# Splitting part of the middle stage's weights during the first feed-forward, and an output projection in two passes

## The chip, the core and the metric

The kernel runs on one core of a Trainium2 chip. The metric is the device time of one execution in microseconds. Engines: TensorE (PE, matmuls, results in PSUM), VectorE (DVE), ScalarE (ACT), GpSimd (POOL) and SyncE (SP, which here only issues DMAs). ACT issues DMAs too. Each engine works through its own queue in order, and the engines meet through semaphores.

## The reference, cut to what matters

One layer of a hybrid decoder on 264 tokens: 256 of a prompt and 8 decode tokens. All weights are float32.

```python
x = x + 0.5 * swiglu(rmsnorm(x, n1), f1g, f1u, f1d)      # first feed-forward, 2048 -> 5504 -> 2048
h = rmsnorm(x, nm)
proj = h @ w_in                                          # input projection, 2048 -> 4864
o_att, k_buf, v_buf = attend(q, k, v, sinks)             # window attention, 16 heads
o_rwkv, shift, S = rwkv_time_mix(proj[..., ATT_COLS:], ...)   # RWKV-7, 16 heads
mixed = jnp.concatenate([o_att, o_rwkv], axis=-1)
x = x + mixed @ w_out                                    # output projection, 2048 -> 2048
x = x + 0.5 * swiglu(rmsnorm(x, n2), f2g, f2u, f2d)      # second feed-forward
y = rmsnorm(x, final_norm)
```

## The kernel before, in words

**Numbers.** A float32 weight is taken apart into two parts that PE reads in its fast format (float32r): hi is the rounded weight, lo what is left. The activations are split in the same way, and each 128 x 128 weight tile meets the 264 tokens in three matmuls, hi with hi, hi with lo and lo with hi, all into one PSUM bank. `mm` (L73) issues them.

**A chunk.** Weights come in chunks of up to four tiles (`CH = 4`, 128 x 512, 256 KB). `chunk` (L115 to L124) loads a chunk with an SP DMA into `raw` (six buffers), casts it on ACT into `hi` (L122, four buffers) and subtracts on DVE into `lo` (L57 through `tt`, four buffers). `gemm` asks for the chunks of one output tile one after another and issues 12 matmuls for each. In the input projection the third chunk of each output tile (`LOP`, k = 8) has its subtraction on POOL. `chunk` runs with high priority in the planner that orders each engine's queue, so loads and splits stand as early as buffers allow. The planner works on the whole program: what stands where in a queue follows from its own estimate of time, not from the order of the Python text.

**First feed-forward** (`ffn`): 43 tiles of the hidden width in six parts; for each part the gate and up products (two times 16 k tiles, 8 chunks for each hidden tile), then the down product for 16 output tiles in two chunks each. That makes 43 x 8 + 16 x 12 = 536 chunks. `early` issues two cache copies of 1016 KB, DRAM to DRAM, on ACT's queue in the third and fourth part. At the end the residual `x` is stored to DRAM (`xsp`) and comes back before the output projection.

**Middle stage** (`mixing_body`): 38 output tiles of the input projection (`win`), four chunks each. Tiles 0 and 1 are the low-rank columns, tiles 2 to 25 the r, k and v columns of eight head pairs, tiles 26 to 37 the attention's k, v and q. After each chunk `tick` moves a list of generators on by one step: `prep` for each head pair, `chain` for each of four batches of two pairs (a triangular solve on DVE in 30 steps of two operations, with tiles going through DRAM scratch: `gm` to `sa`, `sa` to `X` and `Xt`, `Xt` to `sb`, `sb` to `TT`, all on SP's queue), `dec_rwkv` for the decode tokens, `attend` for eight head groups, and `dec_attend`.

**Output projection.** `PASS` lists which of the 16 k tiles each pass takes: six RWKV pairs, then eight attention tiles, then the last two RWKV pairs. Before each pass `drain(need(ks))` runs the generators that make its tiles; a pass with RWKV pairs also needs the decode part. In each pass every one of the 16 output tiles is a gemm over the pass's k tiles, and DVE adds its result to the residual; in the last pass each residual tile is also split and squared for the next norm. Six k tiles make chunks of four and two, two make one chunk of two: 80 chunks in all. The rows of `w_out` are laid out on the host in the order of `PASS`.

Of the kernel before, what the change touches and what calls it, by code (L numbers as in the profile page):

```python
# [7 lines left out]
F32 = mybir.dt.float32  # L8
F32R = mybir.dt.float32r
AF = mybir.ActivationFunctionType  # L10
ALU = mybir.AluOpType
AX = mybir.AxisListType

P = 128
# [4 lines left out]
KD = 16  # L19
# [8 lines left out]
CH, NRAW, NHL = 4, 6, 4  # L28
# [5 lines left out]
LOP = (8,)  # L34
PW = (2, 1, 3, 2, 2)
ALPHA = math.exp(-0.5)
LKV = 26
SEQ = [("b", i) for i in range(4)] + [("kv", i) for i in range(4)] + [("q", i) for i in range(8)]
PASS = [[0, 1, 2, 3, 4, 5], [8, 9, 10, 11, 12, 13, 14, 15], [6, 7]]

VG1, VGM, VG2, VGF = 0, 16, 32, 48
VMU, VKK, VKA, VA0, VRK, VLW, VLB, VSK, VSD = 64, 90, 98, 106, 114, 122, 130, 138, 154
# [4 lines left out]
def body(tc, I, O):  # L47
    nc = tc.nc
    V, A, G, TE, SP = nc.vector, nc.scalar, nc.gpsimd, nc.tensor, nc.sync
    cnt = [0]  # L50

    def uid(s):
        cnt[0] += 1
        return f"{s}{cnt[0]}"

    def tt(e, out, a, b, op):
        return e.tensor_tensor(out=out, in0=a, in1=b, op=op)  # L57
# [32 lines left out]
    def pause(n):  # L90
        for _ in range(n):
            yield

    with ExitStack() as ctx:
        cp = ctx.enter_context(tc.tile_pool(name="cp", bufs=1))
        sp = ctx.enter_context(tc.tile_pool(name="sp", bufs=1))
        wp = ctx.enter_context(tc.tile_pool(name="wp", bufs=1))
        pp = ctx.enter_context(tc.tile_pool(name="pp", bufs=1, space=bass.MemoryType.PSUM))
        dp = ctx.enter_context(tc.tile_pool(name="dp", bufs=1, space=bass.MemoryType.DRAM))
# [12 lines left out]
        def mp():  # L112
            return pp.tile([P, 512], F32, tag="m", bufs=NM, name=uid("m"))

        def chunk(src, n, e, ahead=True):  # L115
            w = n * P
            with tc.high_priority() if ahead else nullcontext():
                raw = wp.tile([P, CH * P], F32, tag="raw", bufs=NRAW, name=uid("raw"))
                hi = wp.tile([P, CH * P], F32R, tag="hi", bufs=NHL, name=uid("hi"))
                lo = wp.tile([P, CH * P], F32R, tag="lo", bufs=NHL, name=uid("lo"))  # L120
                SP.dma_start(raw[:, :w], src)
                A.copy(hi[:, :w], raw[:, :w])  # L122
                tt(e, lo[:, :w], raw[:, :w], hi[:, :w].bitcast(F32), ALU.subtract)
            return hi, lo  # L124

        def gemm(ps, src, xs, step=None, rng=None, pool=False, ahead=True):
            n = len(xs)
            for k0 in range(0, n, CH):
                k1 = min(n, k0 + CH)
                if rng and k0 not in rng:  # L130
                    continue
                hi, lo = chunk(src[:, k0 * P:k1 * P], k1 - k0, G if pool and k0 in LOP else V, ahead)
                for k in range(k0, k1):
                    xh, xl = xs[k]
                    c = slice((k - k0) * P, (k - k0 + 1) * P)
                    mm(ps[:, :T], hi[:, c], xh, k == 0, False)
                    mm(ps[:, :T], hi[:, c], xl, False, False)
                    mm(ps[:, :T], lo[:, c], xh, False, k == n - 1)
                if step:
                    step()  # L140

        vec = cp.tile([P, NVEC], F32, name="vec")
        C = cp.tile([P, 640], F32, name="C")
# [54 lines left out]
        def ffn(nrm, xr, gu, dn, nxt, load=None):  # L198
            rstd = None
            f0 = 0  # L200
            for pi, nf in enumerate(PARTS):
                hs = [None] * nf
                late = []
                if load:
                    early(pi)
                first = load and pi == 0
                if first:
                    banks = [acc() for _ in range(NACC)] + [mp() for _ in range(NM)]
                    n0 = len(banks) // 2
                    for k in range(CH):  # L210
                        load(k)
                    for k0 in range(0, KD, CH):
                        xs = nrm.xs + [None] * (KD - len(nrm.xs))
                        for i, ps in enumerate(banks):
                            gemm(ps, gu[i // 2, i % 2], xs, rng=(k0,), ahead=False)
                            if i >= len(banks) - CH and k0 + CH < KD:
                                load(k0 + CH + i - len(banks) + CH)
                    for f in range(n0):
                        raw = [tmp(), tmp()]
                        V.tensor_copy(raw[0], banks[2 * f][:, :T])  # L220
                        A.copy(raw[1], banks[2 * f + 1][:, :T])
                        late.append((f, *raw))
                for f in range(f0 + n0 if first else f0, f0 + nf):
                    pgu = [acc(), acc()]
                    if first and f == n0:
                        sq = iter(range(KD))

                        def step():
                            for k in [x for _, x in zip(range(2), sq)]:
                                nrm.square(xr[k], k % 2, True)  # L230
                    else:
                        step = None
                    for ps, w in zip(pgu, (gu[f, 0], gu[f, 1])):
                        gemm(ps, w, nrm.xs, step)
                    last = f == f0 + nf - 1
                    if rstd is None:
                        rstd = nrm.rstd(tmp())
                    late.append((f, *(x[:, :T] for x in pgu)))
                    now = [late.pop()] + late[:(len(late) if last else 1)]
                    late = [] if last else late[1:]  # L240
                    for j, pg, pu in now:
                        E = V if last else G
                        g = tmp()
                        tt(V, g, pg, rstd, ALU.mult)
                        s = tmp()
                        act(s, g, AF.Silu)
                        u = tmp()
                        tt(V, u, pu, rstd, ALU.mult)
                        tt(E, u, u, s, ALU.mult)
                        hi, lo = tmp(dt=F32R), tmp(dt=F32R)  # L250
                        A.copy(hi, u)  # L251
                        tt(E, lo, u, hi.bitcast(F32), ALU.subtract)
                        hs[j - f0] = (hi, lo)
                if pi == len(PARTS) - 1:
                    nrm.xs = None
                for o in range(KD):
                    ps = acc()
                    gemm(ps, dn[o, :, f0 * P:(f0 + nf) * P], hs)
                    stt(xr[o], ps[:, :T], 0.5, xr[o], ALU.mult, ALU.add)
                    if pi == len(PARTS) - 1:  # L260
                        nxt(o)
                f0 += nf

        def first_ffn(n2):
            n1 = Norm(VG1)
            xr = []
            A.dma_start(vec, I["vec"])
            def load(k0):
                n1.split(xr[k0], k0 >= CH)

            def nxt(o):
                n2.split(xr[o])
                n2.square(xr[o])
                A.dma_start(xsp[o], xr[o])

            with tc.tile_pool(name="f1", bufs=1) as fp:
                cur[0] = (fp, NH)
                for q in range(4):
                    xg = fp.tile([P, 4, T], F32, tag="x", bufs=4, name=uid("x"))
                    for j in ((0, 2), (2, 4)) if q == 0 else ((0, 4),):  # L280
                        A.dma_start(xg[:, j[0]:j[1]], I["xT"][:, q * 4 + j[0]:q * 4 + j[1], :])
                    xr += [xg[:, j] for j in range(4)]
                ffn(n1, xr, I["gu1"], I["dn1"], nxt, load)

        def mixing(n2, n3):
            with tc.tile_pool(name="mx", bufs=1) as mx:
# [3 lines left out]
        def mixing_body(mx, n2, n3):  # L290
# [29 lines left out]
            mixed = [None] * 16  # L320
            have = [False]

            def win(t):
                ps = acc()
                gemm(ps, I["win"][t], n2.xs, tick, pool=True)
                if not have[0]:
                    n2.rstd(rs)
                    have[0] = True
                return ps
# [486 lines left out]
            for kind, i in SEQ:  # L816
# [10 lines left out]
                elif kind == "kv":  # L827
                    w, p = i // 2, i % 2
                    ps = win(LKV + i)
# [34 lines left out]
            k0 = 0  # L864
            for pi, ks in enumerate(PASS):
                drain(need(ks))
                for k in ks:
                    split(k)
                for o in range(KD):
                    ps = acc()  # L870
                    gemm(ps, I["wout"][o, :, k0 * P:(k0 + len(ks)) * P], [mixed[k] for k in ks], tick)
                    with tc.high_priority():
                        tt(V, xr[o], ps[:, :T], xr[o], ALU.add)
                    if pi == len(PASS) - 1:
                        n3.split(xr[o])
                        n3.square(xr[o])
                for k in ks:
                    mixed[k] = None
                k0 += len(ks)
# [132 lines left out]
```

## Time and profile before

| what | value |
|---|---|
| three runs, median (lowest to highest) | 2129.2 us (2127.75 to 2129.91) |
| the profiled execution | 2127.34 us, of which the span from first to last instruction is 2125.2 |
| granted PE clock, mean over the span | 0.970 |
| busy share of the span | PE 96%, DVE 63%, ACT 49%, POOL 20% |
| data moved | 356.27 MB, 168 GB/s on average |

The stages by their own times: the first loads of the input projection are issued at 757.7 us, its last at 1124.1, and the second feed-forward begins at about 1366.

```profile
0.00:757.00 757.00, 747.09 (x6114) 745.82 (x6115) 453.00 (x768) 373.28 (x672) 91.99 (x94) 1.00 0.59 188
757.00:1140.00 383.00, 354.57 (x3182) 332.25 (x3180) 297.16 (x657) 205.44 (x425) 190.84 (x326) 0.96 0.47 136
...
1250.00:1366.00 116.00, 112.51 (x947) 108.54 (x947) 81.14 (x164) 62.09 (x134) 17.99 (x27) 0.99 0.54 171
1366.00:2125.00 759.00, 745.63 (x6125) 744.80 (x6123) 435.87 (x736) 365.96 (x651) 94.09 (x91) 0.99 0.55 178
```

Each line is a stretch of time (from, to, length in us), the busy us of PE, of PE's weight loads, DVE, ACT and POOL with their instructions, the share of the PE clock that was granted, the mean busy share of the 16 DMA engines and the GB/s that they moved. A group line, as the prediction shows them, gives the code line, engine, operation, the tile written and the tiles read, the count, and then the busy us, the mean ns of one, the idle time of the engine just before them and what ended it. A wait line gives the engine and line that waited, for whom, the total us, how often and the longest.

### The profile page before, as it was taken

How to read it: one execution, taken by the hardware profiler on the slowest of the kernel's cores; microseconds unless marked ns; L12 is line 12 of the kernel's file. 1: busy time of each engine (PE TensorE's matmuls, PEld its weight loads, DVE VectorE, ACT ScalarE, POOL GpSimd, SP SyncE). 2: the span in 40 equal slices, each digit the busy share in tenths (PEclk: the TensorE clock that was granted, in tenths of full speed). 3: DMA queues.
4: the chain of work that ended last, by engine and by line, in shares of the span. 5: the costliest groups of instructions: out<-in, count | busy, mean ns of one | idle time of the engine just before them, and what ended most of it. 6: DMA issues, size and time to landing. Idle time of an engine off the chain costs nothing.

```text
span 2125.2 us, 45168 instructions
## 1 busy us (share of the span) xinstructions
PE 2043.9 (96%) x16870; PEld 1995.4 (94%) x16870; DVE 1334.3 (63%) x2551; ACT 1045.8 (49%) x2002; POOL 419.5 (20%) x581
## 2 busy tenths in 40 slices
PE   8999999999999999989996899999999999999997
PEld 8999999999999999888885679899999999999997
DVE  5765555556555677766888646755555565555555
ACT  5644444444444566546542344644444444444445
POOL 0301011010201146533454201220110102011012
PEclk9999999999999999989997579999999999999999
DMA  6565565656555574434343145456555565555554
GB/s 224 176 182 182 175 205 175 207 180 183 181 177 185 185 227 139 122 96 135 112 136 114 41 138 186 156 182 181 181 175 187 177 184 181 177 186 176 186 176 140
DMA packets 227532, 356.27 MB, mean 168 GB/s; under 512 B 42176, under 2 KB 83152, under 8 KB 227280
## 3 DMA queue, kind: packets, MB, share of 16 engines
q1 hardware_dynamic: 221616, 344.72, 51.8%
q10 hardware_dynamic: 5696, 8.66, 1.1%
q8 instruction: 132, 2.16, 0.4%
q14 instruction: 88, 0.72, 0.1%
HBM read 345.15 MB, written 10.21 MB: 167 GB/s over the span
## 4 chain that ended last, share of the span: by engine, by line
PE 86%; DVE 7%; DMA 2%; ACT 1%; issue 1%; POOL 1%; SPq 1%; DVEq 0%; POOLq 0%; ACTq 0%
PE acc L73 79%; PE m L73 6%; DVE lo L57 1%; DMA raw<-in_gu 1%; DVE Xt L57 1%; DVE st L57 1%; ACT L67 1%; DVE ld L57 0%; ACT t L67 0%; DMA sb<-Xt 0%; DVE s L60 0%; DVE t L57 0%; DMA TT<-sb 0%; DVE TT L57 0%; DVE t L64 0%
## 5 line engine op out<-in xcount | busy, mean ns | idle before, releaser
L73 PE MATMUL acc<-s,hi 128*128 128x264 f32 x7072 | 1317.5, 286 | 10.0 <-ACT hi L122 8.3
L57 DVE TENSOR_TENSOR lo<-raw,hi 128x512 fp32r<-128x512 f32 (+1 forms) x1266 | 861.7, 684 | 600.6 <-ACT hi L122 578.7
L122 ACT CAST hi<-raw 128x512 fp32r<-128x512 f32 (+2 forms) x1304 | 780.5, 602 | 909.5 <-PE acc L73 830.6
L73 PEld LDWEIGHTS acc<-s,hi 128*128 128x128 f32 x7072 | 1108.8, 190 | 17.8 <-ACT hi L122 8.5
L73 PE MATMUL acc<-s,lo 128*128 128x264 f32 x3536 | 1016.1, 288 | 12.7 <-DVE lo L57 10.5
L73 PEld LDWEIGHTS acc<-s,lo 128*128 128x128 f32 x3536 | 669.9, 189 | 18.5 <-DVE lo L57 14.1
L73 PE MATMUL acc<-t,hi 128*128 128x264 f32 x2752 | 502.7, 284 | 1.6 <-ACT t L251 1.6
L73 PEld LDWEIGHTS acc<-t,hi 128*128 128x128 f32 x2752 | 426.0, 188 | 1.9 <-ACT t L251 1.8
L57 POOL TENSOR_TENSOR t<-t,t 128x264 f32<-128x264 f32 (+1 forms) x162 | 173.0, 1068 | 1209.6 <-ACT hi L122 897.6
L73 PE MATMUL acc<-t,lo 128*128 128x264 f32 x1376 | 388.2, 284 | 0.0
L73 PEld LDWEIGHTS acc<-t,lo 128*128 128x128 f32 x1376 | 258.2, 188 | 0.0
L57 DVE TENSOR_TENSOR t<-acc,t 128x264 f32<-128x264 f32 x164 | 70.9, 433 | 36.7 <-PE acc L73 36.5
L57 POOL TENSOR_TENSOR s<-s,s 128x264 f32<-128x264 f32 (+1 forms) x56 | 49.5, 886 | 195.8 <-ACT s L67 179.1
L57 POOL TENSOR_TENSOR lo<-raw,hi 128x512 fp32r<-128x512 f32 x38 | 49.7, 1308 | 57.4 <-ACT hi L122 57.2
L67 ACT ACT_TABLE_LOAD x42 | 53.9, 1283 | 1.9 <-PEq L1004 1.2
L60 DVE SCALAR_TENSOR_TENSOR s<-acc,s 128x264 f32<-128x264 f32 x96 | 40.7, 428 | 16.8 <-PE acc L73 16.3
L60 DVE SCALAR_TENSOR_TENSOR x<-acc,x 128x264 f32<-128x264 f32 x96 | 40.6, 427 | 10.9 <-PE acc L73 10.4
L57 DVE TENSOR_TENSOR st<-X,Xt 128x60 f32<-128x60 f32 (+10 forms) x120 | 36.1, 300 | 10.1 <-DMA Xt<-sa 7.4
L67 ACT ACTIVATE t<-t 128x264 f32<-128x264 f32 x94 | 40.0, 425 | 3.3 <-DVE t L57 1.8
L57 DVE TENSOR_TENSOR Xt<-Xt,st 128x60 f32<-128x60 f32 (+10 forms) x120 | 36.7, 305 | 1.7
L251 ACT CAST t<-t 128x264 fp32r<-128x264 f32 x86 | 35.5, 413 | 3.6 <-POOL t L57 2.1
L73 PE MATMUL m<-s,hi 128*128 128x264 f32 x160 | 30.1, 287 | 0.4 <-ACT hi L122 0.4
(209 smaller groups left out, 1116.5 us busy)
## 6 DMA issues: line engine op xcount, KB each, us to landing
raw<-in_gu SPq DMA_DIRECT2D x688, 256.0 KB, 3.2
raw<-in_dn SPq DMA_DIRECT2D x224, 256.0 KB, 2.7
raw<-in_win SPq DMA_DIRECT2D x152, 256.0 KB, 3.2
raw<-in_dn SPq DMA_DIRECT2D x160, 192.0 KB, 2.7
raw<-in_wout SPq DMA_DIRECT2D x48, 256.0 KB, 3.0
raw<-in_wout SPq DMA_DIRECT2D x32, 128.0 KB, 2.4
xsp<-x ACTq DMA_DIRECT2D x16, 132.0 KB, 3.5
s<-xsp SPq DMA_DIRECT2D x16, 132.0 KB, 3.0
```

What stands on the lines that cost most here:

```text
L57: return e.tensor_tensor(out=out, in0=a, in1=b, op=op)
L60: return V.scalar_tensor_tensor(out=out, in0=a, scalar=s, in1=b, op0=op0, op1=op1)
L67: return A.activation(out=out, in_=in_, func=f, **k)
L73: TE.matmul(out, lhsT, rhs, start=start, stop=stop, **k)
L122: A.copy(hi[:, :w], raw[:, :w])
L251: A.copy(hi, u)
```

## The change

Of the middle stage's weight chunks 104 are split during the first feed-forward, written to DRAM as hi and lo side by side, and read back as such where they are needed.

- `hi` and `lo` of a chunk become one tile `hl` (four buffers as before).
- `presplit` is a generator over 72 chunks of the input projection (tiles 2 to 25, k = 0, 4 and 12; not k = 8, whose subtraction is on POOL) and the second chunk of each output tile in both output passes (2 x 16). For each it loads 256 KB into `praw` (three buffers) on SP, casts on ACT and subtracts on DVE into `phl` (three buffers), and stores 512 KB from ACT's queue into a DRAM tile of its own. `gemm` moves it on by one step for each chunk of the first feed-forward, and an item takes four steps (`PSTEP`).
- `chunk` with `done` given loads the 512 KB straight into `hl` on SP's queue: no `raw`, no cast, no subtraction.
- `PASS` has two passes of eight k tiles in place of three: all RWKV pairs, then attention. That makes 64 chunks, all of four tiles.

```diff
+PRE, PREK = range(2, 26), (0, 4, 12)
+PSTEP = 4
-PASS = [[0, 1, 2, 3, 4, 5], [8, 9, 10, 11, 12, 13, 14, 15], [6, 7]]
+PASS = [[0, 1, 2, 3, 4, 5, 6, 7], [8, 9, 10, 11, 12, 13, 14, 15]]
...
-        def chunk(src, n, e, ahead=True):
+        def chunk(src, n, e, ahead=True, done=None):
             w = n * P
             with tc.high_priority() if ahead else nullcontext():
-                raw = wp.tile([P, CH * P], F32, tag="raw", bufs=NRAW, name=uid("raw"))
-                hi = wp.tile([P, CH * P], F32R, tag="hi", bufs=NHL, name=uid("hi"))
-                lo = wp.tile([P, CH * P], F32R, tag="lo", bufs=NHL, name=uid("lo"))
-                SP.dma_start(raw[:, :w], src)
-                A.copy(hi[:, :w], raw[:, :w])
-                tt(e, lo[:, :w], raw[:, :w], hi[:, :w].bitcast(F32), ALU.subtract)
+                hl = wp.tile([P, 2, CH * P], F32R, tag="hl", bufs=NHL, name=uid("hl"))
+                hi, lo = hl[:, 0], hl[:, 1]
+                if done is not None:
+                    SP.dma_start(hl[:, :, :w].bitcast(F32), done)
+                else:
+                    raw = wp.tile([P, CH * P], F32, tag="raw", bufs=NRAW, name=uid("raw"))
+                    SP.dma_start(raw[:, :w], src)
+                    A.copy(hi[:, :w], raw[:, :w])
+                    tt(e, lo[:, :w], raw[:, :w], hi[:, :w].bitcast(F32), ALU.subtract)
             return hi, lo
...
+        def presplit(fp):
+            todo = [("win", t, k, CH) for t in PRE for k in PREK]
+            k0 = 0
+            for ks in PASS:
+                if len(ks) > CH:
+                    todo += [("wout", o, k0 + CH, len(ks) - CH) for o in range(KD)]
+                k0 += len(ks)
+            for i, (nm, t, k, n) in enumerate(todo):
+                w = n * P
+                raw = fp.tile([P, CH * P], F32, tag="praw", bufs=3, name=uid("praw"))
+                hl = fp.tile([P, 2, CH * P], F32R, tag="phl", bufs=3, name=uid("phl"))
+                tc.keep_in_program_order(SP.dma_start(raw[:, :w], I[nm][t, :, k * P:k * P + w]))
+                A.copy(hl[:, 0, :w], raw[:, :w])
+                tt(V, hl[:, 1, :w], raw[:, :w], hl[:, 0, :w].bitcast(F32), ALU.subtract)
+                d = dp.tile([P, 2, w], F32, tag=f"pre{i}", name=f"pre{i}")
+                A.dma_start(d, hl[:, :, :w].bitcast(F32))
+                ready[nm, t, k] = d
+                yield from pause(PSTEP)
...
-                hi, lo = chunk(src[:, k0 * P:k1 * P], k1 - k0, G if pool and k0 in LOP else V, ahead)
+                done = ready.get((pre[0], pre[1], pre[2] + k0)) if pre else None
+                hi, lo = chunk(src[:, k0 * P:k1 * P], k1 - k0, G if pool and k0 in LOP else V, ahead, done)
...
+                for g in side:
+                    next(g, None)
...
+                side.append(presplit(fp))
                 ffn(n1, xr, I["gu1"], I["dn1"], nxt, load)
+                for _ in side.pop():
+                    pass
...
-                gemm(ps, I["win"][t], n2.xs, tick, pool=True)
+                gemm(ps, I["win"][t], n2.xs, tick, pool=True, pre=("win", t, 0))
...
-                    gemm(ps, I["wout"][o, :, k0 * P:(k0 + len(ks)) * P], [mixed[k] for k in ks], tick)
+                    gemm(ps, I["wout"][o, :, k0 * P:(k0 + len(ks)) * P], [mixed[k] for k in ks], tick,
+                         pre=("wout", o, k0))
```

More of the change, by code (lines that the diff above doesn't have):

```diff
@@ L126, in gemm @@
-        def gemm(ps, src, xs, step=None, rng=None, pool=False, ahead=True):
+                hl = wp.tile([P, 2, CH * P], F32R, tag="hl", bufs=NHL, name=uid("hl"))
[7 more added lines that the diff above has]
+                    tt(e, lo[:, :w], raw[:, :w], hi[:, :w].bitcast(F32), ALU.subtract)
@@ new lines, in chunk @@
+            return hi, lo
+        ready = {}
+        side = []
+        def presplit(fp):
[16 more added lines that the diff above has]
+                yield from pause(PSTEP)
@@ L127, in gemm @@
+        def gemm(ps, src, xs, step=None, rng=None, pool=False, ahead=True, pre=None):
             n = len(xs)
```

## The prediction

> **What bounds the kernel now.** I read four views: busy time by stage, what TensorE (PE) waited for, the costliest groups, and the DMA rows. Columns of the stages: window, its length, then busy us (instructions) of PE, weight loads, VectorE (DVE), ScalarE (ACT), GpSimd (POOL), then the granted PE clock, the DMA engines' busy share and GB/s.
>
> ```profile
> core 0: us, PE busy (x) PEld busy (x) DVE busy (x) ACT busy (x) POOL busy (x), PEclk, DMA share, GB/s
> 100.00:600.00 500.00, 498.22 (x4094) 497.53 (x4093) 287.56 (x486) 234.51 (x413) 52.80 (x49) 1.00 0.58 185
> ...
> 760.00:1000.00 240.00, 225.31 (x1871) 212.91 (x1871) 171.93 (x344) 136.22 (x271) 122.08 (x231) 0.94 0.48 138
> 1000.00:1140.00 140.00, 126.27 (x1290) 116.35 (x1288) 122.66 (x309) 66.95 (x150) 67.81 (x94) 0.98 0.46 131
> 1140.00:1250.00 110.00, 84.06 (x510) 64.02 (x509) 67.14 (x228) 39.02 (x123) 24.64 (x43) 0.61 0.23 65
> ...
> 860.00:880.00 20.00, 15.29 (x116) 13.49 (x116) 19.64 (x47) 6.68 (x14) 14.31 (x27) 0.99 0.42 130
> ```
>
> Both feed-forwards are PE-bound at full clock: 4094 matmuls in 500 us is 0.122 us each, so a chunk of four weight tiles (12 matmuls) takes 1.465 us. The middle stage is where time can be won: from 760 to 1000 PE is idle 14.7 us and the clock of 0.94 costs another 225.3 x 0.06 = 13.5 us. Where a chain's triangular solve runs (860 to 880) DVE is full and PE starves. After 1000 come the input chunks 26 to 37, which the change does not pre-split, and from 1140 the last chain and attention, where DVE is not full and the clock is low: latency, which the change does not touch.
>
> What PE waited for between 760 and 1000 (total us, times, longest):
>
> ```profile
> PE m L73 <- DVE gm L57: 5.3, 4, 3.1
> PE acc L73 <- DVE lo L57: 4.3, 3, 3.1
> PE m L73 <- DVE Xt L57: 2.8, 1, 2.8
> PE acc L73 <- POOL lo L57: 1.9, 2, 1.5
> ```
>
> The splits are named only for 4.3 us; gm and Xt are chain steps that share DVE's queue with splits. From 740 to 1370 the split groups cost (busy us, mean ns, idle before):
>
> ```profile
> L57 DVE TENSOR_TENSOR lo<-raw,hi 128x512 fp32r<-128x512 f32 x183 | 140.0, 769 | 53.6 <-ACT hi L122 49.2 <-PE m L73 2.0
> L122 ACT CAST hi<-raw 128x512 fp32r<-128x512 f32 x221 | 135.3, 619 | 156.3 <-PE acc L73 130.9 <-DVE st L57 5.7 <-DVE t L57 5.6
> ```
>
> DMA: size and time to landing, then stretches of the first feed-forward and of the last output pass.
>
> ```profile
> raw<-in_win SPq DMA_DIRECT2D x152, 256.0 KB, 3.2
> sa<-gm SPq DMA_DIRECT2D x32, 16.0 KB, 2.1
> ...
> DMA to landing us min/median/max: 2.8/3.2/4.8
> ...
> 10.00:15.00 5.00, 4.66 (x30) 4.66 (x31) 1.90 (x4) 1.64 (x5) 0.00 (x0) 1.00 1.03 407
> 15.00:20.00 5.00, 5.00 (x43) 5.00 (x42) 4.46 (x9) 4.73 (x10) 0.00 (x0) 1.00 0.51 157
> ...
> 278.00:280.00 2.00, 2.00 (x18) 2.00 (x18) 0.15 (x1) 0.00 (x0) 0.00 (x0) 1.00 0.31 133
> ...
> 282.00:284.00 2.00, 1.78 (x13) 1.48 (x13) 1.42 (x3) 1.59 (x3) 0.00 (x0) 1.00 0.73 209
> ...
> 1350.00:1355.00 5.00, 3.85 (x25) 2.97 (x23) 5.00 (x11) 4.89 (x12) 3.07 (x4) 1.00 0.59 204
> ```
>
> The third line is for `raw<-in_win` alone. A full DMA moved 407 GB/s; PE near 283 us ran out once, behind a 1 MB cache copy issued at 271.7; the short last output pass is DVE-bound (5.00 of 5).
>
> **The first feed-forward.** 104 items are added, one per four chunks, so they end after 416 of 536 chunks, 610 us. One item: a 256 KB load on SP, an ACT cast (0.62), a DVE subtract (0.69 in this stage), a 512 KB store issued on ACT (0.33, as a load's issue). Per 5.86 us ACT goes from 47% to 63%, DVE from 58% to 69%. PE stays covered: a split starts when the chunk four earlier frees its buffer, 5.86 us ahead, and needs 0.62 + 0.69; the 4.5 us left is what an ACT wait for an item's load, or for DVE before its store, may take. Queued behind such a wait are the next casts, and behind them PE. POOL's queue gets nothing. Cost 0.
>
> DMA demand goes from 185 GB/s by (256 + 512) KB per 5.86 us = 134 to 319 GB/s. Against 407 that is 78%; by the share that bytes take in this stage (0.58 for 185) it would be 1.00. The full-load row is nearer, since queued loads run back to back there; 78%, cost 0, with rival B for the other end. The two cache copies of 1 MB fall into these 610 us; in the first one DVE and ACT had nothing to split for 4 us (278 row) and PE lost 0.2. With 78% behind it the backlog lasts longer: 1 MB at 407 GB/s is 2.6 us, the most that each can cost if nothing hides it; I take 1 each: +2 (0 to +5).
>
> Start: ACT is nearly full from 15 to 20 (4.73 of 5), and two items (2 x 0.95) come into it, with their loads (0.65 each at 407) ahead of chunks 1 and 5 in SP's queue: +1.5 (0 to +4).
>
> **The input projection, chunks of tiles 2 to 25.** 72 splits leave: 72 x 0.769 = 55 us of DVE's 172, 72 x 0.62 = 45 of ACT's 136. The 4.3 us on lo go. Of gm and Xt (8.1) I take two thirds, because DVE is full just where they occur: 5.4. That is 9.7 of 14.7 idle; the same share of the slow clock would be 9, and I take half, 4.5, since chain matmuls also run in slow spells. Together -14 (0 to -28, all idle and clock). In the built program the chains stand some four chunks earlier among the gemms than before, which agrees but proves nothing.
>
> The new wait: each of the 72 loads is 512 KB straight into one of the four matmul buffers, and SP issues it only when PE has freed that buffer. Before, six raw buffers ahead of four split ones gave ten chunks of cover; now it is four. A turn of a buffer takes 1.465 (PE) + 0.33 (issue) + landing. Landing: 3.2 for 256 KB, plus 256 KB at 407 GB/s = 0.65, so 3.9; from the minimum 3.5, from the maximum 5.5. At 3.9 a turn is 5.7, under PE's 5.86 for four chunks: no cost. The fourth chunk of each tile (POOL's) keeps its raw buffers and is loaded six tiles ahead. What is behind the wait in SP's queue matters too: the chain stores and reloads (gm to scratch, scratch to X, Xt, TT) stand between two of these loads. Such a group waits 2.1 for a landing and issues eight DMAs (2.6): 4.7 + 3.9 = 8.6 against 7.3, the five chunks that PE has left when the last buffer before the group came free: 1.3 late, five times in this range, half covered by chain matmuls: +3 (0 to +14.5 at 5.5).
>
> **Output projection.** The number of big matmuls stays (16 x 16 x 3). Both versions drain the last chain before the first pass in the built order, so merging heads 6 and 7 into pass one adds no wait. The last pass of two k tiles, 0.73 us of PE against two DVE passes and a split each, goes: PE idle from 1340 to 1365 is 3.3 us (3.85 of 5 in the row): -3.3 (-5 to 0). Half the chunks are then loaded split, on two of the four buffers; at 5.7 a turn no cost. After that the second feed-forward is untouched.
>
> **Sum.** +2 + 1.5 - 14 + 3 - 3.3 = -10.8. The profiled execution took 2127.3 (span 2125.2 and 2.1 around it): 2116.5. It lies 1.9 under the median of the runs, 2129.2, so I predict 2118.
>
> **Rivals.** A, the other side: landing under load. From 4.1 us a turn exceeds 5.86. At 4.7, halfway from median to maximum, the output passes (16 turns, no chain matmuls in between) lose 16 x 0.64 = 10 and the five SP groups 5 x 2.1 = 10.5; the input tiles, spaced 6.6 us or more by their issue times, lose nothing. In place of my +3 that is +21: 2136. At 5.5 it is 23 + 14.5 + 5.5 for eight dense tiles: 2158. The gain is eaten from about 4.4 us. For it: the maximum of 4.8, and a buffer that was ten chunks deep. Against it: the median, and a mean DMA share of 0.48 here. The Trainium skill (DMA: Bandwidth & Descriptors, section Latency and other measured facts) speaks for A: HBM access takes 0.2 us on average and 2 us at high load, so by its figures landing would grow by up to 1.8, an estimate of 5.7 us and a time beyond A's far end; the trace bears it out only in part, 2.8 to 4.8 for the same load.
>
> B: the first feed-forward becomes DMA-bound (share 1.00 by its own bytes). A shortfall of 2% over 610 us is 12, and the copies cost 2.6 each instead of 1: +15 on my sum: 2133. Against it: 407 GB/s.
>
> C: chain latency, not DVE's queue, makes gm, Xt and the slow clock; then only 4.3 of the 14 comes: 2128. For it: lo is named for little. Against it: DVE at 19.64 of 20.
>
> **How the numbers follow.** Forecast 0.50, A 0.23, C 0.17, B 0.10. About 0.2% (4.3 us) can be told from no change, so faster 0.50, same 0.17 (C), slower 0.33 (A and B). The forecast's own range is 2104 to 2125; with A up to a landing of 5.0 (15 + 12 + 1.6 in place of 3: 2144) and C and B inside, 2100 to 2146.
>
> **What would show it.** PE at 1.00 and fully busy from 100 to 740, DMA share near 0.8 there (near 1.0 with splits waiting for raw: B). Between 760 and 1000 few waits on gm, Xt and lo (C if they stay). Waits of PE on DMA hl: a few us in total, landing near 3.9 (A if tens of us, above all in the output passes). No DVE-full stretch at the end of the output projection. I am wrong if the middle is not shorter by some 12 us or the first feed-forward grows by more than 6.

## The result, and the profile after

The changed kernel takes 2200.4 us (median of four runs, 2196.04 to 2205.25), against 2128.9 for the kernel before: ratio 1.0333, 95% interval 1.0317 to 1.0349. The forecast was 2118, and the range ended at 2146. The profiled execution took 2199.5, with a span of 2197.7; 72.5 us of span came on top. By the start times of matmuls in the two traces they came like this:

| stretch | before | after | difference |
|---|---|---|---|
| first feed-forward, to its last down product | 767.4 us | 844.5 us | +77.1 |
| from there to the second feed-forward's first down product | 683.2 us | 677.0 us | -6.2 |
| from there to the last down product | 659.6 us | 661.2 us | +1.6 |

So the first feed-forward, costed at nothing but a slower start and two copies, lost twelve times what the middle gained. The stretches below are the first feed-forward, then the four of the middle that the prediction began with, each 77 us later than before, and the last output pass. Columns as before.

```profile
core 0: us, PE busy (x) PEld busy (x) DVE busy (x) ACT busy (x) POOL busy (x), PEclk, DMA share, GB/s
100.00:600.00 500.00, 465.33 (x3643) 453.43 (x3642) 304.18 (x517) 238.80 (x443) 36.59 (x40) 0.98 0.87 287
...
837.00:1077.00 240.00, 220.68 (x1875) 207.16 (x1874) 118.72 (x273) 96.59 (x204) 106.04 (x232) 0.97 0.68 211
1077.00:1217.00 140.00, 129.38 (x1281) 119.85 (x1281) 125.25 (x308) 64.65 (x145) 70.09 (x94) 0.98 0.48 140
1217.00:1327.00 110.00, 91.41 (x522) 69.06 (x520) 66.72 (x228) 37.33 (x120) 26.38 (x44) 0.60 0.26 76
1327.00:1443.00 116.00, 115.30 (x993) 112.76 (x992) 56.22 (x105) 44.55 (x94) 17.42 (x26) 1.00 0.76 244
```

From 100 to 600 PE issued 3643 matmuls where it had issued 4094: 11% of its work is missing, while DVE (61%), ACT (48%) and the DMA engines (share 0.87) all have time left. A stretch that slows with nothing full is one where something waits in turns.

In the input projection DVE fell from 172 to 119 us, as meant, and the clock rose from 0.94 to 0.97; yet the 240 us hold 1875 matmuls against 1871. What PE waited for there:

```profile
PE acc L75 <- DMA hl<-pre: 15.0, 11, 3.2
PE m L75 <- DVE st L59: 2.0, 1, 2.0
PE m L75 <- DVE gm L59: 1.5, 1, 1.5
```

The waits on lo, gm and Xt (12.4 us before) are down to 1.5, with 2.0 on `st`, another step of the chain; 15.0 us of waits for the read-backs stand in their place.

Now the first feed-forward. What ACT waited for from 20 to 680 us of the changed kernel (total us, times, longest):

```profile
ACT phl L146 <- DMA praw<-in_win: 127.4, 55, 5.3
ACT phl L146 <- DMA praw<-in_wout: 61.9, 29, 4.4
ACT hl L127 <- PE acc L75: 49.5, 76, 1.3
ACT hl L127 <- DMA raw<-in_gu: 19.7, 14, 6.6
```

Before, ACT's large wait, from 100 to 740, was for PE to free a buffer: it was ahead, and the wait was slack.

```profile
ACT hi L122 <- PE acc L73: 312.9, 411, 3.8
```

Now 189.3 us go into the cast of an item that waits for its own load. One turn of it, in ACT's queue and in SP's (start, us, instruction; in brackets the idle time before it and what ended it), and PE in the same microseconds:

```profile
537.54 1.02 ACT L127 CAST hl<-raw 128x512 fp32r<-128x512 f32 x2
542.97 0.62 ACT L146 CAST phl<-praw 128x512 fp32r<-128x512 f32 x1 [4.42 <-DMA praw<-in_wout]
543.50 0.61 ACT L127 CAST hl<-raw 128x512 fp32r<-128x512 f32 x1
```

```profile
537.24 0.79 SPq L145 DMA_DIRECT2D praw<-in_wout  x1
538.13 7.15 SPq L126 DMA_DIRECT2D raw<-in_dn  x4
545.33 0.59 SPq L145 DMA_DIRECT2D praw<-in_wout  x1
```

```profile
536.00:540.00 4.00, 4.00 (x35) 4.00 (x34) 3.03 (x6) 1.90 (x5) 0.00 (x0) 1.00 0.87 287
540.00:544.00 4.00, 2.62 (x22) 2.40 (x20) 0.38 (x1) 1.03 (x2) 0.00 (x0) 1.00 0.73 243
```

The item's load goes out at 537.2 to 538.0. ACT has two casts left ahead of that item's, and then stands still until 543. While it stands, no chunk is cast, DVE has nothing to subtract (0.38 of 4 us), so no raw buffer comes free and SP needs 7.15 us for four loads that take 0.33 each to issue. The next item's load is behind those four, at 545.3, and is late in its turn: ACT waits for it too, until 549.5. PE runs dry at 540 to 544, and the DMA engines, at 243 GB/s, have room to spare. The Trainium skill (Perfetto Trace Analysis, section Tensor Engine Instruction) says that ACT and DVE take their instructions strictly first in, first out; the trace agrees: the cast at 543.50 starts only when the late one, 0.53 us earlier, is under way.

The loss grows as long as there are items. By the issue times of the chunk loads in the two traces, the changed kernel is 25 us behind at chunk 100, 45 at 200, 58 at 300 and 76 at 400; after 420, with the last item done, it stays at 77 to 78.

The DMA rows of the changed kernel from 100 to 600 us (KB, median us to landing) show why an item's load is not there in time:

```profile
raw<-in_gu SPq DMA_DIRECT2D x187, 256.0 KB, 5.3
pre<-phl ACTq DMA_DIRECT2D x78, 512.0 KB, 4.2
...
praw<-in_win SPq DMA_DIRECT2D x57, 256.0 KB, 5.5
...
praw<-in_wout SPq DMA_DIRECT2D x22, 256.0 KB, 5.9
```

Over the whole run an item's 256 KB land in 5.6 us (median; 4.2 to 11.5). The chunks' own loads have slowed too, from 3.2 us in the same stretch of the kernel before to 5.3, but six raw buffers let SP send them far ahead of their casts. In the built order an item's cast stands 3.7 chunk casts behind its load on the mean (1 to 6; 3.8 by the order in the trace), 5.4 us at PE's 1.465 a chunk. Distance here counts the chunk casts that ACT does between the freeing of the raw buffer that the last load ahead of the item's goes into and the item's cast.

### The profile page after: what moved, and what is told of

The parts are those of the page before. It is cut to its first block, busy times and chain, and to the rows that moved or that the text cites. A ratio compares the mean times of both kernels' runs of the same rounds, so it can differ in the third digit from the quotient of the medians.

```text
span 2197.7 us, 44956 instructions
## 1 busy us (share of the span) xinstructions
PE 2078.3 (95%) x16870; PEld 2011.3 (92%) x16870; DVE 1342.5 (61%) x2519; ACT 1020.4 (46%) x1984; POOL 372.4 (17%) x581
## 4 chain that ended last, share of the span: by engine, by line
PE 65%; DMA 17%; DVE 10%; ACT 3%; issue 3%; SPq 1%; POOL 0%; ACTq 0%; DVEq 0%; POOLq 0%
PE acc L75 59%; DMA praw<-in_win 8%; PE m L75 6%; DVE hl L59 3%; DMA praw<-in_wout 3%; DMA hl<-pre 2%; DMA raw<-in_gu 2%; ACT hl L127 1%; ACT phl L146 1%; DVE st L59 1%; DVE Xt L59 1%; DVE t L59 1%; DVE x L62 0%; DMA raw<-in_win 0%; DMA Xt<-sa 0%
## 5 line engine op out<-in xcount | busy, mean ns | idle before, releaser
L75 PE MATMUL acc<-s,hl 128*128 128x264 f32 x10608 | 1359.7, 288 | 58.9 <-ACT hl L127 30.6
L75 PEld LDWEIGHTS acc<-s,hl 128*128 128x128 f32 x10608 | 1321.5, 190 | 82.4 <-ACT hl L127 34.8
L59 DVE TENSOR_TENSOR hl<-raw,hl 128x512 fp32r<-128x512 f32 x1146 | 812.0, 716 | 446.5 <-ACT hl L127 438.3
L127 ACT CAST hl<-raw 128x512 fp32r<-128x512 f32 (+1 forms) x1184 | 706.7, 605 | 712.4 <-PE acc L75 577.5
L75 PE MATMUL acc<-t,hl 128*128 128x264 f32 x4128 | 515.2, 286 | 18.1 <-ACT hl L127 11.3
L75 PEld LDWEIGHTS acc<-t,hl 128*128 128x128 f32 x4128 | 507.7, 189 | 24.5 <-ACT hl L127 13.4
L59 POOL TENSOR_TENSOR t<-t,t 128x264 f32<-128x264 f32 (+1 forms) x162 | 135.2, 834 | 1305.4 <-DVE t L59 891.4
L59 DVE TENSOR_TENSOR phl<-praw,phl 128x512 fp32r<-128x512 f32 x104 | 72.4, 696 | 173.7 <-ACT phl L146 163.8
L146 ACT CAST phl<-praw 128x512 fp32r<-128x512 f32 x104 | 64.4, 620 | 191.9 <-DMA praw<-in_win 129.7
L59 POOL TENSOR_TENSOR hl<-raw,hl 128x512 fp32r<-128x512 f32 x38 | 49.9, 1312 | 77.2 <-ACT hl L127 69.4
```

The source lines that it names most:

```text
L75: TE.matmul(out, lhsT, rhs, start=start, stop=stop, **k)
L146: A.copy(hl[:, 0, :w], raw[:, :w])
```

## The experiments

The theory, Q in the expectations: the cast of an item stands too close behind its load in ACT's queue, and SP's queue closes the loop. Its rival there, theory D: the DMA engines became the bound (the prediction's rival B).

**The passes alone.** The kernel before, with the two passes.

```diff
-PASS = [[0, 1, 2, 3, 4, 5], [8, 9, 10, 11, 12, 13, 14, 15], [6, 7]]
+PASS = [[0, 1, 2, 3, 4, 5, 6, 7], [8, 9, 10, 11, 12, 13, 14, 15]]
```

> The kernel before with the output projection in two passes, nothing split early. If the third pass of two k tiles cost what its idle PE showed, the time falls by 3.3 us (ratio 0.9985, 0.9975 to 1.000) and PE has no idle stretch at the end of the output projection. If merging the last two RWKV tiles into the first pass makes that pass wait for the last chain, it rises instead (over 1.002).

Measured: 2126.28 against 2129.51, ratio 0.9982 (0.9973 to 0.9991), by the ratio 3.8 us less. The term of -3.3 holds.

**The cast pinned.** The changed kernel; the item's cast is held at its place in the program's order, as its load is.

```diff
-                A.copy(hl[:, 0, :w], raw[:, :w])
+                tc.keep_in_program_order(A.copy(hl[:, 0, :w], raw[:, :w]))
```

> The changed kernel with one edit: the cast of an early item is kept where it stands in the program, six chunks behind the load's neighbours instead of 3.7 on average. Same bytes, same instructions. Theory Q (queue loop): ACT stands in its queue waiting for an item's load that was issued too shortly before, and while it waits the next loads are not issued; then the first feed-forward ends at 768 to 780 us instead of 844, and the time is 2125 to 2140. Theory D (DMA-bound: 319 GB/s is more than the DMA engines give beside this work): it still ends at 830 or later and the time stays above 2185.

Measured: 2128.86, ratio 0.9997 (0.9986 to 1.0007); the first feed-forward ends at 778.4. One moved instruction per item takes back 66 of the 77 us. Up to the end of the first feed-forward nearly all else stands as it did: apart from the items' own instructions SP's 544 chunk loads are in the same order in both traces, and so is POOL's queue; of ACT's 712 other instructions 34 have moved, of DVE's 783 it is 12. In the built order the cast now stands 6.0 chunk casts behind its load, 8.8 us. The same stretch, and what ACT waited for from 20 to 680, in this kernel:

```profile
100.00:600.00 500.00, 494.95 (x4046) 493.51 (x4046) 345.44 (x570) 275.74 (x498) 40.69 (x50) 1.00 0.95 321
```

```profile
ACT hl L127 <- PE acc L75: 181.1, 247, 5.4
ACT hl L127 <- DMA raw<-in_gu: 37.3, 31, 5.9
...
ACT phl L146 <- DMA praw<-in_win: 4.2, 11, 0.6
```

ACT waits for PE again, and the DMA engines move 321 GB/s, more than in the slow kernel: their limit was not reached there. The item loads landed no sooner (5.9 us median); the distance to the cast decided, not the load.

**No store.** The changed kernel without the store to DRAM; the middle stage splits all its chunks itself.

```diff
-                d = dp.tile([P, 2, w], F32, tag=f"pre{i}", name=f"pre{i}")
-                A.dma_start(d, hl[:, :, :w].bitcast(F32))
-                ready[nm, t, k] = d
```

> The changed kernel whose early items are loaded and split but not stored; the middle stage splits all its chunks itself. It leaves out the 512 KB stores and the reading back. DMA demand in the first feed-forward is 230 GB/s instead of 319. The cast of an item stands only 2.4 chunks behind its load here. Theory Q: ACT still waits for item loads, and the first feed-forward still ends late, 785 to 830 us. Theory D: it ends at 767 to 772 as before.

Measured: one time, 2257.63; the first feed-forward ends at 918.5. Two thirds of the added bytes are gone, and the loss has doubled: Q's direction, and further than either theory had it. An item's load lands sooner here (4.4 us median), but without the store the built order puts the cast only 2.4 chunk casts, 3.5 us, behind it:

```profile
100.00:600.00 500.00, 436.44 (x3202) 412.93 (x3201) 255.99 (x451) 204.94 (x395) 40.60 (x44) 0.96 0.60 182
```

```profile
ACT phl L146 <- DMA praw<-in_win: 218.8, 67, 7.2
```

At a DMA share of 0.60 the stretch loses 22% of its matmuls. So the loss here is not a bound in the DMA engines.

**The traffic alone.** The item's load and a store of the same size from a constant tile, without cast and subtraction; the middle stage splits all its chunks itself.

```diff
-                A.copy(hl[:, 0, :w], raw[:, :w])
-                tt(V, hl[:, 1, :w], raw[:, :w], hl[:, 0, :w].bitcast(F32), ALU.subtract)
...
-                A.dma_start(d, hl[:, :, :w].bitcast(F32))
-                ready[nm, t, k] = d
+                tc.keep_in_program_order(A.dma_start(d, full))
```

> The changed kernel with the DMA traffic of the early items alone: 104 loads of 256 KB and 104 stores of 512 KB of a constant tile at the same pace, no casts and no subtractions of them; the middle stage splits all its chunks itself. Theory Q: the first feed-forward ends at 768 to 778 us. Theory D: at 830 or later, as in the changed kernel.

Measured: one time, 2121.41 (below the kernel before, since the two passes and the one tile for hi and lo are in it); the first feed-forward ends at 777.3, at 319 GB/s:

```profile
100.00:600.00 500.00, 494.15 (x4029) 492.92 (x4028) 295.30 (x479) 229.12 (x406) 37.87 (x48) 0.99 0.94 319
```

The added traffic as such costs 10 us of the 77. Mean distance in chunk casts against loss of the first feed-forward is now a series: 2.4 and 151 us, 3.7 and 77, 6.0 and 11. In time the cast stands 3.5, 5.4 and 8.8 us behind a load that lands in 4.4, 5.6 and 5.9. The three kernels differ in more than this distance (the first has no store), but rival B is out as the cause of the 77.

Two more, to see what the read-backs cost in the middle.

**A ring of five.** The pinned kernel with five matmul buffers, paid for with two raw buffers, and each item's load issued an item ahead.

```diff
-CH, NRAW, NHL = 4, 6, 4
+CH, NRAW, NHL = 4, 4, 5
...
-                raw = fp.tile([P, CH * P], F32, tag="praw", bufs=3, name=uid("praw"))
+                if i + 1 < len(todo):
+                    fetch(i + 1)
+                raw = raws[i]
```

> The kernel with the pinned cast, with five matmul buffers instead of four, four raw buffers instead of six (the memory of one for the other), and an item's load issued one item ahead, so that its cast keeps its distance. Theory H (in the dense input tiles the read-back halves come just in time: a turn of four buffers is longer than PE's four chunks): PE's waits on the read-back fall from 15 us to under 7, tiles 2 to 9 take 57 to 59 us instead of 62, and the time is 3 to 8 us under the pinned cast's. Rival S (what holds the loads is SP's queue, with the chain's stores and reloads, not the number of buffers): waits and time stay within 2 us.

Measured: 2188.09, ratio 1.0277 (1.0255 to 1.03), where theory H had it 3 to 8 us under the pinned kernel. Two results in one. PE's waits on read-backs fall from 15.4 us in the pinned kernel to 4.1, and the middle (measured as in the table below) from 618.9 to 609.2. But the first feed-forward ends at 845.2: here ACT waits for the chunks' own loads.

```profile
ACT hl L127 <- DMA raw<-in_gu: 179.3, 135, 8.6
ACT hl L127 <- DMA raw<-in_dn: 83.9, 66, 3.4
```

Its item casts stand 8 chunk casts behind their loads, so this is another cause than the changed kernel's. Four raw buffers are too few under the added traffic, though the second feed-forward, with the same four and without it, loses nothing.

**From tile 10.** The pinned kernel; tiles 2 to 9, which PE runs through without chain work in between, keep their own splits (80 items).

```diff
-PRE, PREK = range(2, 26), (0, 4, 12)
+PRE, PREK = range(10, 26), (0, 4, 12)
```

> The kernel with the pinned cast, with input tiles 10 to 25 split early instead of 2 to 25: 80 items instead of 104. Theory H: tiles 2 to 9 fall back to 56 to 58 us from 62, the rest keeps its gain, and the time falls by 4 to 7 us against the pinned cast. Rival R (relief of DVE and ACT in tiles 2 to 9 is worth as much as the read-back costs): no change there, the time within 2 us.

Measured: 2120.87, ratio 0.996 (0.9945 to 0.9975). Tiles 2 to 9 go from 61.9 to 56.4 us, and the waits on read-backs from 15.4 to 9.9. The dense tiles were dearer with read-backs than with their own splits.

The first feed-forward still lost 9 to 11 us: by when each raw load was issued, in the pinned kernel some 6 by chunk 60, and the rest where the two cache copies run.

**A late start, copies at the end.** The pinned kernel; the items begin 32 chunks later, and both copies stand in the sixth part, behind the last item.

```diff
+            yield from pause(PWAIT)
...
-            elif pi in (2, 3):
-                nm, ck = (("ks", "ck"), ("vs", "cv"))[pi - 2]
+            elif pi == 5:
+                for nm, ck in (("ks", "ck"), ("vs", "cv")):
```

> The kernel with the pinned cast, with the first item 32 chunks later and both 1 MB cache copies after the last item instead of among them. Theory T (what is left of the first feed-forward's loss, 11 us, is the start and the two copies that meet the added traffic): it ends at 768 to 771 us instead of 778, the time is 7 to 11 us lower, 2118 to 2122. Rival U (the loss is spread over the whole stage, by the traffic as such): the end moves by less than 3 us.

Measured: 2126.16, ratio 0.9985 (0.9973 to 0.9997), the end at 776.2: a move of 2 us, which by the number is rival U's outcome. By the issue times it is not U's mechanism: until chunk 450 the items cost 2 to 3 us; then the two copies, back to back and with no item beside them, cost 7.

**Late start and from tile 10.** Both edits above.

> The late start and the input tiles from 10 on together. By theories H and T the gains add: 2112 to 2118 us, ratio to before 0.992 to 0.995. If U or R holds, 2122 to 2130.

Measured: 2116.76, ratio 0.9941 (0.9924 to 0.9957), as expected in the time. But the first feed-forward ends at 777.9, no sooner than the pinned kernel's (the copies, back to back, cost 8 here).

**Copies apart.** The last kernel with one copy in the fifth part and one in the sixth (`elif pi in (4, 5)`).

> Late start, input tiles from 10 on, and the two 1 MB cache copies in the fifth and sixth part of the first feed-forward, after the last item (80 items end by chunk 352, the copies are issued from about 360 and 448) and 88 chunks apart. If the 7 us that the copies cost in the late start came of their standing back to back, the first feed-forward ends at 768 to 772 us and the time is 2107 to 2113. If a copy costs its 2.6 us and more wherever it stands, it ends at 774 or later and the time stays at 2114 to 2119.

Measured: 2114.06, ratio 0.9918 (0.9899 to 0.9937); the first feed-forward ends at 771.0, 3.6 over the kernel before. The end is where it was expected, the time 1 us above its range.

**Five buffers, copies apart.** The last kernel with `NHL` of 5, and raw buffers taken from each stage's own memory: six in the feed-forwards, four in the middle.

> The same with five matmul buffers, and the raw buffers given by each stage's own memory: six in the feed-forwards, four in the middle stage. By theory H the waits on the read-back fall under 5 us from 11 and the middle stage is 2 to 6 us shorter than with four. Against it: the raw buffers of a stage can be filled only when the memory of the stage before is free, which can cost some us at each change of stage; then it is slower than the copies apart by 2 us or more.

Measured: 2117.38, ratio 0.9936 (0.9918 to 0.9955). No gain, and the expectation's caution is what happened. PE's waits on read-backs are 5.1 us against 7.9 with the copies apart, and the first feed-forward ends sooner (768.2). But the raw buffers now belong to the stage: the input projection's first loads are issued at 771.05, after that end, and PE starts on it 6.7 us after its last down product, where it was 0.1. So the input projection begins 3.8 us later in all.

**No items at all.** The changed kernel with an empty list of items: what is left of the change is the two passes, and hi and lo in one tile.

```diff
+            todo = []
```

> The changed kernel with no early item at all: two passes, and hi and lo of a chunk in one buffer. If the early split is worth what the waits on DVE showed (some 9 us net in the middle), this is at the two passes' time, 2124 to 2128. If the middle stage is set by chain latency and a favourable order, and the early split buys nothing, it is as fast as the best version with items, 2108 to 2118.

Measured: 2108.82, ratio 0.9892 (0.987 to 0.9915). By its median it is the fastest of all the kernels (its interval overlaps that of the copies apart): no version above has a gain that its side edits, the two passes and the one tile, don't give alone. What PE waited for in it from 770 to 1010:

```profile
PE acc L75 <- DVE hl L59: 5.3, 3, 2.9
PE m L75 <- DVE N L59: 2.9, 1, 2.9
PE m L75 <- DVE TN L540: 1.9, 2, 1.7
PE m L75 <- DVE gm L59: 1.6, 2, 1.1
```

The waits on lo (here `hl` from DVE) are as before, since every chunk is split on the spot. Those on gm (5.3 before) and Xt (2.8) are down to 1.6, but `N` and `TN`, later steps of the same chain, take 4.8: the chain's waits have moved more than they have gone, and this view does not show where the gain comes from.

**One tile alone.** The kernel before with hi and lo of a chunk in one tile, three passes.

```diff
-                hi = wp.tile([P, CH * P], F32R, tag="hi", bufs=NHL, name=uid("hi"))
-                lo = wp.tile([P, CH * P], F32R, tag="lo", bufs=NHL, name=uid("lo"))
+                hl = wp.tile([P, 2, CH * P], F32R, tag="hl", bufs=NHL, name=uid("hl"))
+                hi, lo = hl[:, 0], hl[:, 1]
```

> The kernel before, three passes, with hi and lo of a chunk in one buffer and nothing else. Two passes gave a ratio of 0.998 alone and 0.989 together with the one buffer. If the gain is the one buffer's (hi and lo freed together, so the planner sets another order), the ratio here is 0.989 to 0.994. If the two only work together, it is 0.996 to 1.002.

Measured: 2119.67 against 2128.92, ratio 0.9965 (0.9951 to 0.9978): within the range of "only together", at its lower end, and yet a gain clear of none.

The middle of these kernels, by matmul times of one profiled execution each (us; single executions of one kernel differ by some us, and that of the passes alone was the fastest of its runs). "To tile 2" ends with the first matmul of tile 2 and so holds PE's wait for the first read-back, 3.15 us in the changed kernel:

| stretch | before | after | passes alone | one tile alone | no items | copies apart |
|---|---|---|---|---|---|---|
| to tile 2 | 12.6 | 15.9 | 12.6 | 12.6 | 12.6 | 12.6 |
| tiles 2 to 9 | 56.6 | 64.4 | 56.6 | 56.4 | 56.4 | 56.5 |
| tiles 10 to 25 | 185.2 | 176.4 | 182.5 | 176.8 | 177.7 | 175.4 |
| tiles 26 to 37 | 222.2 | 218.5 | 223.0 | 221.2 | 219.3 | 217.6 |
| to 300 matmuls into the second feed-forward | 149.6 | 144.5 | 143.0 | 149.2 | 141.7 | 145.0 |
| sum | 626.2 | 619.7 | 617.7 | 616.2 | 607.7 | 607.1 |

## Why the prediction was wrong, point by point

**The step that failed: the first feed-forward's items at "Cost 0".** The working said that the 4.5 us left of a split's lead "is what an ACT wait for an item's load, or for DVE before its store, may take", and named what is queued behind such a wait. It then booked nothing, without setting the item's landing against the place of its cast in ACT's queue, and it priced each wait once. Two things were missing. The landing under this load is 5.6 us, and the cast stood 5.4 us behind its load on the mean, so most items came late (84 waits for 104 items). And the wait feeds itself: SP's loads wait for the subtractions behind the late cast, and the next item's load is queued behind those loads. So the lead was not lost once and rebuilt, but worn down item after item: 77 us over some 416 chunks. The pinned cast, which changes nothing else in the text, shows it: -66 us. High busy shares were not the cause: in the pinned kernel from 100 to 600 DVE is 69% busy, as worked out, ACT 55% without the DMA issues, and the DMA engines move 321 GB/s, while PE is busy 494.95 of 500 us.

**Start and copies**, taken at 1.5 (0 to 4) and 2 (0 to 5). Mis-sized, by less: start and traffic together cost from 2 to 3 us with the late start to some 6, the two copies 6 to 8 us in all: 5.6 in the pinned kernel, 7.6 with the traffic alone, 7 back to back. Rival B had 15 us on top of these two terms; with the traffic alone 10 came in all, at the start and behind the copies and not spread over the stage. The DMA engines delivered 319 to 321 GB/s with PE near its pace, as the forecast had it; their busy share is then 0.94 to 0.95, nearer to B's 1.00 from bytes than to the 78%, so here a share near 1 was not a bound.

**Input tiles, -14 for the relief and +3 for the new wait.** Measured for tiles 2 to 25: -1.0 (241.8 to 240.8), or +2.3 with the longer stretch to tile 2, where -11 was forecast. The waits on lo, gm and Xt did go, but PE waited 15.0 us for read-backs; the +3 is the term mis-sized here. And "no items" gains nearly as much in tiles 10 to 25 without a single early split: 185.2 against 177.7, and 175.4 with the splits done early. So the relief of DVE is worth some 2 us there, less than single executions differ by, and rival C's doubt (only part of the 14 comes) was right; whether chain latency, its mechanism, is the reason is not shown. What shortened these tiles, by single executions, was the one tile for hi and lo, which the prediction put at nothing without a word: alone it takes tiles 10 to 25 to 176.8.

**Rival A's mechanism is there, its place is not.** Landing of the read-backs was 4.5 us median (3.1 to 10.4) where the forecast had 3.9, beyond the 4.4 from which A ate the gain, and a fifth buffer took PE's waits down from 15.4 to 4.1 us. But they lay in the input projection, above all the dense tiles 2 to 9 (+7.8 us, where A at 4.7 had nothing), and in the output passes, where A expected 10, they are 0.5. By the difference between "after" and "no items" the early split makes the middle 12.0 us longer (619.7 against 607.7; one execution each).

**Output projection, -3.3.** Right: -3.8 alone. In the stretch without a chain the profile after shows PE busy 115.3 of 116.

**What would show it**, as the prediction had it: the middle shorter by some 12, and the first feed-forward longer by no more than 6. It is 6.2 and 77; both fail.

**Left open.** Why an item's 256 KB land a little later than a chunk's. Why one tile for hi and lo helps (the planner then places the chain's steps otherwise, but that is argued and not shown), and why it gives more with the two passes (0.9892) than the product of both alone (0.9947) by the times; the profiled executions of the table, in which the parts add up (-8.5, -10.0, -18.5), cannot decide it.

## What to carry to other kernels

Work that is moved into a stage with idle engines is not priced by busy shares: for each moved instruction that waits for a load, set its distance behind that load in its engine's queue, in the stage's own work units, against the landing time under the new load. If the loads of the stage wait for what is queued behind it, a late one makes the next one late, and the cost is a rate and not an offset. And run the change without its headline part: here the two side edits were the whole gain, and the early split turned 2108.8 us into 2200.4.

## What the runs showed of the hardware

From 100 to 600 us a chunk's 256 KB of gate and up weights landed in 3.2 us (median) in the kernel before, at 185 GB/s, and in 5.3 in the changed one, at 287 GB/s; an item's 256 KB landed in 5.5 to 5.9 there. Loads and stores together reached 321 GB/s at a DMA share of 0.95 with PE busy 494.95 of 500 us at a clock of 1.00. Two DRAM-to-DRAM copies of 1016 KB, one right behind the other and nothing added beside them, cost PE 7 to 8 us; one apiece in two parts, with the late start, the whole first feed-forward lost 3.6.
